# Attention output projection turned to channels on the partitions, and a second buffer for one tile of the S5 preparation

## The chip, the cores and the metric

The kernel runs on one core of a Trainium2 chip. The metric is the device time of one execution in microseconds; three executions of the kernel before were timed. One further execution was taken with the profiler and gives the trace that is quoted here.

## What is computed

One block on x of 1024 tokens by 1024 channels, in fp32. Cut to its main lines:

```python
h = rms_norm(x, norm1_g)
q, k, v, g_ret, u, g_s5 = split(h @ w_in)
ret = retention(rotary(q), rotary(k), v) * silu(g_ret)      # 8 heads, chunks of 128
ssm = s5_branch(u, ...) * silu(g_s5)                        # 64 groups of 16, state 64
x = x + concat([ret, ssm]) @ w_out
qa = rms_norm(x, norm2_g) @ xa_wq                           # 4 heads of 256
ka, va = m @ xa_wk, m @ xa_wv                               # m: 256 memory rows, normed
p = softmax(qa @ ka.T / 16)
x = x + (p @ va) @ xa_wo
return rms_norm(x, norm_f_g)
```

The S5 branch is computed with tables built from its parameters: powers of the state matrix, and the B and C matrices multiplied with them.

## The kernel before

Every projection is done in split precision: `mm3` (L100 to L103) issues three matmuls (high by high, high by low, low by high) for each block of 128 contracted channels. Weights come in groups of 256 columns through `load_w` (L71): SP issues two loads into `wraw`, ScalarE (ACT) copies the high part `whi`, VectorE (DVE) or GpSimd (POOL) subtracts the low part `wlo`. `get_w` always loads one group ahead.

The program's order is set by a list scheduler of the tile framework, separately for each engine: it uses its own durations, and every engine then works strictly in that order. SP issues nearly all DMAs, in order, so that one issue that waits holds all behind it. Tiles come from pools with a fixed number of buffers (`bufs`); a write waits until the readers of the buffer's last use are done.

The stages are: norm, then the loop `for i in range(4)` over pairs of retention heads (L612, about 0 to 400 us), then the u projection and S5 scan, the gates and the two parts of `w_out`, memory keys and values, queries and scores, and last the output projection `w_xo`.

**S5 preparation in the loop.** In the loop's iterations 1 to 3 a hook (`s5_hook`, L504) is called at fixed places. For each of 16 blocks b, `s5_prep(b)` (L457) computes W1 and VV on DVE with one product t1 on POOL (L476), and `s5_finish(b)` (L484) transposes W1 on TensorE (PE) into PSUM, `mps`, L488, and multiplies VV with B1, `kps`, L495. For each pair of blocks `s5_tables(ct)` (L422), ct 0 to 7, builds a 512 KB table on POOL by doubling (`tab`, L426 to L326), stores it with SP to `tab_d` (L430), stores a block of zeros from `z` (L432, L433), and computes B1, B2 and C1 on POOL (L447 to L454). `tab` and B1 have one buffer each, so the next `tab` waits for the store of the last, and the next B1 for the `kps` matmuls that read the last. The profile and the order drop digits from names: `B` is B1 on L447 to L450 and B2 on L451 to L453, `t` on L476 is t1, `C` is C1. In the order's rows a first number is the ct or the block b, and a last one is the tile's own number.

**The loop's other work around it.** `rope_load` (L296) copies the projected queries or keys from PSUM and swaps 32-row blocks with four SP DMAs (`sw_q`, `sw_k`, L303). `rope_turn` (L306) multiplies and adds on DVE (L309 to L311). `ret_store` (L593) transposes the retention output of the iteration before (`rtps`, L599), scales it on DVE (`rt`, L601) and stores it to `ret_d` (L604). `mps`, `kps`, `rtps` and other small PSUM tiles share one pool of four buffers.

**Output projection.** `wo_half(half, ...)` (L1020) works on 512 tokens. Tokens stand on the PSUM partitions: the attention output `o` is the stationary operand and 256 weight columns move, 768 matmuls of 128x256 over both halves. x1 lies in DRAM with channels on the partitions, so 64 PE transposes (`pxps`, L1038) and ACT copies turn it. DVE adds (L1048), ACT squares with a running sum along the row (L1050), and `finish` (L1057 to L1069) takes the reciprocal root for each 128 tokens, scales and stores. `attend(1, gi)` is interleaved with half 0. The lines around the sum:

```python
mm3(ps[:, t, 0:256], oT[k][0][:, ts], oT[k][1][:, ts], hi[:, k, :], lo[:, k, :], k == 0, k == 7)
v.tensor_tensor(x2[:, cs], ps[:, t, 0:256], x2[:, cs], ALU.add)
s.activation(jk, x2[:, cs], AF.Square, accum_out=ssq[t0 + t][:, gi:gi + 1])
```

Of the kernel before, what the change touches and what calls it, by code (L numbers as in the profile page):

```python
# [41 lines left out]
GELU_S = math.sqrt(2.0 / math.pi)  # L42
CONST_PAD, SSM_PAD, SB_PAD, KA_PAD, QA_PAD, PP_PAD, WO_OFF = 56, 16, 16, 8, 16, 48, 0


@with_exitstack
def block_kernel(ctx: ExitStack, tc: tile.TileContext, a: dict):
# [15 lines left out]
    def sm_ps(shape, name="smps"):  # L63
        return psm.tile(shape, F32, tag="sm", name=name)
# [82 lines left out]
    g2, gm, glu_b, invf, rsgn, nsgn, psgn = (off[z] for z in ("g2", "gm", "glu_b", "invf", "rsgn", "nsgn", "psgn"))  # L147
    d4, i16 = off["d4"], off["i16"]
    g1 = gp1
# [272 lines left out]
    def s5_tables(ct):  # L422
# [12 lines left out]
        sh = [P, 2, GB, 16]  # L435
        B1 = pr.tile([P, 2 * GB + 1, 16], F32, tag="B1", name=f"B1_{ct}")
        B2 = pr.tile([P, 2 * GB, 16], F32, tag="B2", name=f"B2_{ct}")
        C1 = pr.tile([P, 2 * GB, 16], F32, tag="C1", name=f"C1_{ct}")
        tt = pr.tile([P, 2, GB, 16], F32, tag="tt16", name=f"tt16_{ct}")
# [4 lines left out]
        def hg(x):  # L444
            return x.rearrange("p (h g) q -> p h g q", h=2)
# [7 lines left out]
        g.tensor_tensor(b2, b2, tt, ALU.subtract)  # L453
        g.tensor_scalar(hg(C1), raw[:, :, 2], psgn, None, op0=ALU.mult)  # L454
        per_ct[ct] = raw, B1, B2, C1

    def s5_prep(b):  # L457
        gs = slice(b * GB, b * GB + GB)
        ct, hb = b // 2, b % 2
        if hb == 0:  # L460
            s5_tables(ct)
        raw, B1, B2, C1 = per_ct[ct]
        ks = slice(hb * GB, hb * GB + GB)
        raw, B2, C1 = raw[:, hb], B2[:, ks], C1[:, ks]
# [12 lines left out]
        v.tensor_tensor(W1, W1, t1, ALU.add)  # L477
        v.tensor_tensor(VV, pw(PR, 9), ve(C1, 9), ALU.mult)
        v.tensor_tensor(t2, pw(PI, 9), ve(raw[:, 3], 9), ALU.mult)
# [539 lines left out]

    def wo_half(half, oT, between):  # L1020
        on = [qap.tile([P, D], F32, tag=("qhi", "qlo")[t % 2], name=f"on{half}{t}") for t in range(4)]
        ssq = [small.tile([P, 5], F32, tag=f"ssq{t}", name=f"ssq{half}{t}") for t in range(4)]
        pre = [z[:, 4:5] for z in ssq]
        for gi in range(4):
            hi, lo = get_w("w_xo", gi)
            xts = []
            for c in range(2):
                xt = pp.tile([P, 512], F32, tag="xt", name=f"xt{half}{gi}{c}", bufs=4)
                nc.sync.dma_start(out=xt, in_=a["x1_d"][2 * gi + c][:, half * 512:half * 512 + 512])
                xts.append(xt)  # L1030
            between(gi)
            cs = slice(gi * 256, gi * 256 + 256)
            for t0 in range(0, 4, 2):
                px = sm_ps([P, 2, 256], "pxps")
                for t in range(2):
                    ts = slice((t0 + t) * P, (t0 + t + 1) * P)
                    for c in range(2):
                        nc.tensor.transpose(px[:, t, c * P:c * P + P], xts[c][:, ts], ident)  # L1038
                    s.activation(on[t0 + t][:, cs], px[:, t, :], AF.Copy)
                ps = big_ps([P, 2, 512], "wops")  # L1040
                for t in range(2):
                    ts = slice((t0 + t) * P, (t0 + t + 1) * P)
                    for k in range(8):
                        mm3(ps[:, t, 0:256], oT[k][0][:, ts], oT[k][1][:, ts], hi[:, k, :], lo[:, k, :],
                            k == 0, k == 7)
                for t in range(2):
                    x2 = on[t0 + t]
                    v.tensor_tensor(x2[:, cs], ps[:, t, 0:256], x2[:, cs], ALU.add)  # L1048
                    jk = pp.tile([P, 256], F32, tag="jk", name="jk", bufs=2)
                    s.activation(jk, x2[:, cs], AF.Square, accum_out=ssq[t0 + t][:, gi:gi + 1])  # L1050
                    if gi < 3:
                        v.tensor_tensor(x2[:, cs], x2[:, cs], gf[:, cs], ALU.mult)
                    if gi == 2:
                        v.tensor_reduce(pre[t0 + t], ssq[t0 + t][:, 0:3], axis=AX.X, op=ALU.add)
                        v.tensor_scalar(pre[t0 + t], pre[t0 + t], 1.0 / D, EPS, op0=ALU.mult, op1=ALU.add)
                    if gi == 3:
                        finish(half, t0 + t, x2, ssq[t0 + t][:, 3:4], pre[t0 + t])  # L1057

    def finish(half, t, x2, last, pre):
        ss = small.tile([P, 1], F32, tag="ssf", name="ssf")  # L1060
        rf = small.tile([P, 1], F32, tag="rf", name="rf")
        v.scalar_tensor_tensor(ss, last, 1.0 / D, pre, op0=ALU.mult, op1=ALU.add)
        rsqrt(rf, ss, 1, "f")
        row = (half * 4 + t) * P
        s.activation(x2[:, 0:512], x2[:, 0:512], AF.Copy, scale=rf)
        nc.sync.dma_start(out=a["out"][row:row + P, 0:512], in_=x2[:, 0:512])
        v.scalar_tensor_tensor(x2[:, 768:D], x2[:, 768:D], rf, gf[:, 768:D], op0=ALU.mult, op1=ALU.mult)
        v.tensor_scalar(x2[:, 512:768], x2[:, 512:768], rf, None, op0=ALU.mult)
        nc.sync.dma_start(out=a["out"][row:row + P, 512:D], in_=x2[:, 512:D])  # L1069

# [28 lines left out]
def host_arrays(x, mem, positions, norm1_g, w_in, ret_gn_g, s5_a_re, s5_a_im, s5_log_dt,  # L1099
# [93 lines left out]
```

## Time and profile before

| what | value |
|---|---|
| median of 3 runs | 1151.91 us (1148.85 to 1152.83) |
| the profiled execution's own time | 1150.77 us |
| its span on the core | 1148.7 us |
| PE busy | 1118.4 us (97 %), 6636 matmuls |
| DVE, ACT, POOL busy | 654.8, 436.6, 241.0 us |
| mean granted clock of PE | 0.992 |
| HBM traffic | 122.04 MB read, 44.43 MB written |

The span runs from the first to the last instruction on the core. Times in the trace count from its start. The ends of matmuls are modelled, so the pace of PE is read from the distance between the starts of neighbouring matmuls, not from their durations.

### The profile page before, as it was taken

The page shows a single profiled execution, that of the slowest core. Times are in us where ns is not written, and L with a number is a line of the kernel's source. Part 1 is how long each engine was busy: PE and PEld are TensorE (multiplying, and loading weights), DVE is VectorE, ACT ScalarE, POOL GpSimd, SP SyncE. Part 2 cuts the span into 40 slices and gives each one's busy share as a digit, 9 for nine tenths or more (in the row PEclk, how much of TensorE's full clock was granted, in tenths as well). Part 3 has the DMA queues.
Part 4 walks back from the last instruction along what each step waited for, and adds up shares of the span by engine and source line. Part 5 has one row for each costly group of instructions (what it writes and reads, how often), then busy time and mean ns, then how long its engine had stood idle before and what let it go on. Part 6 is the DMA issues. An engine that isn't in the chain of part 4 may idle for free.

```text
span 1148.7 us, 17497 instructions
## 1 busy us (share of the span) xinstructions
PE 1118.4 (97%) x6636; PEld 966.3 (84%) x6636; DVE 654.8 (57%) x1388; ACT 436.6 (38%) x863; POOL 241.0 (21%) x342
## 2 busy tenths in 40 slices
PE   8999979999999999999999999999999999999996
PEld 6887957888888888887888888888889888889996
DVE  8896664765663445756585145443645555555564
ACT  7331422432432323434453133233334444344453
POOL 2338798452040001111121100002220000000000
PEclk9999989999999999999999999999999999999999
DMA  6413433442342299898794387443346422122251
GB/s 238 125 38 108 132 127 125 141 157 99 87 139 63 76 244 260 263 275 233 213 294 147 120 228 248 155 156 126 121 152 204 171 72 75 54 74 74 97 198 74
DMA packets 92372, 171.81 MB, mean 150 GB/s; under 512 B 10881, under 2 KB 46977, under 8 KB 92289
## 3 DMA queue, kind: packets, MB, share of 16 engines
q1 hardware_dynamic: 92000, 170.57, 47.2%
q8 instruction: 52, 0.85, 0.3%
q14 instruction: 32, 0.25, 0.1%
q10 hardware_dynamic: 288, 0.14, 0.0%
HBM read 122.04 MB, written 44.43 MB: 145 GB/s over the span
## 4 chain that ended last, share of the span: by engine, by line
PE 80%; POOL 8%; DMA 5%; DVE 4%; issue 1%; ACT 1%; SPq 0%; DVEq 0%; POOLq 0%; ACTq 0%
PE wops L101 3%; PE ups L103 3%; PE wops L103 3%; PE wops L102 3%; PE ups L101 3%; PE qaps L103 3%; PE qaps L102 3%; PE qaps L101 3%; PE obps L102 3%; PE ups L102 3%; PE obps L103 3%; PE glups L103 3%; PE obps L101 3%; PE glups L101 3%; PE glups L102 3%; PE gsps L101 2%
## 5 line engine op out<-in xcount | busy, mean ns | idle before, releaser
L102 PE MATMUL vps<-wlo_w_v,hh 128*128 128x256 f32 x256 | 73.0, 285 | 0.7 <-POOL wlo_w_v L81 0.7
L101 PE MATMUL vps<-whi_w_v,hh 128*128 128x256 f32 x256 | 73.0, 285 | 0.6 <-ACT qs_k L299 0.6
L101 PE MATMUL wops<-whi_w_xo,o 128*128 128x256 f32 x256 | 73.4, 287 | 0.0
L103 PE MATMUL vps<-whi_w_v,hl 128*128 128x256 f32 x256 | 73.0, 285 | 0.0
L103 PE MATMUL wops<-whi_w_xo,o 128*128 128x256 f32 x256 | 71.8, 280 | 0.0
L102 PE MATMUL wops<-wlo_w_xo,o 128*128 128x256 f32 x256 | 71.5, 279 | 0.0
L917 POOL TENSOR_TENSOR sq<-sq,sqx 128x1024 f32<-128x1024 f32 x7 | 19.2, 2738 | 195.3 <-ACT sqx L916 195.3
L101 PE MATMUL gsps<-hh,whi_w_gs 128*128 128x512 f32 x128 | 51.1, 399 | 0.0
L101 PE MATMUL gps<-hh,whi_w_g 128*128 128x512 f32 x128 | 51.0, 399 | 0.0
L101 PE MATMUL ups<-hh,whi_w_u 128*128 128x512 f32 x128 | 50.8, 397 | 0.0
L103 PE MATMUL ups<-hh,wlo_w_u 128*128 128x512 f32 x128 | 50.6, 395 | 0.0
L102 PE MATMUL gps<-hl,whi_w_g 128*128 128x512 f32 x128 | 50.6, 395 | 0.0
L102 PE MATMUL gsps<-hl,whi_w_gs 128*128 128x512 f32 x128 | 50.5, 395 | 0.0
L102 PE MATMUL ups<-hl,whi_w_u 128*128 128x512 f32 x128 | 50.4, 394 | 0.0
L103 PE MATMUL gps<-hh,wlo_w_g 128*128 128x512 f32 x128 | 50.4, 393 | 0.0
L103 PE MATMUL gsps<-hh,wlo_w_gs 128*128 128x512 f32 x128 | 50.3, 393 | 0.0
L101 PE MATMUL oaps<-reth,whi_w_oa 128*128 128x512 f32 x128 | 50.3, 393 | 0.0
L103 PE MATMUL qaps<-h,wlo_w_xq 128*128 128x512 f32 x128 | 50.2, 392 | 0.0
L101 PE MATMUL qaps<-h,whi_w_xq 128*128 128x512 f32 x128 | 50.1, 392 | 0.0
L102 PE MATMUL oaps<-retl,whi_w_oa 128*128 128x512 f32 x128 | 50.0, 391 | 0.0
L102 PE MATMUL qaps<-h,whi_w_xq 128*128 128x512 f32 x128 | 50.0, 390 | 0.0
L102 PE MATMUL obps<-ssmlo,whi_w_ob 128*128 128x512 f32 x128 | 49.9, 390 | 0.0
(394 smaller groups left out, 3372.6 us busy)
## 6 DMA issues: line engine op xcount, KB each, us to landing
CS<-tab_d SPq DMA_DIRECT2D x32, 256.0 KB, 5.9
yr<-y_d SPq DMA_DIRECT2D x16, 512.0 KB, 6.9
wraw_w_xq<-w_xq SPq DMA_DIRECT2D x16, 512.0 KB, 4.1
wraw_w_xo<-w_xo SPq DMA_DIRECT2D x16, 512.0 KB, 4.3
vv_d<-VV SPq DMA_DIRECT2D x16, 288.0 KB, 2.6
VV<-vv_d SPq DMA_DIRECT2D x16, 288.0 KB, 5.1
wraw_w_v<-w_v SPq DMA_DIRECT2D x8, 512.0 KB, 4.3
wraw_w_g<-w_g SPq DMA_DIRECT2D x8, 512.0 KB, 5.1
```

Of the source, the lines that this page charges most:

```text
L101: nc.tensor.matmul(out, wh, xh, start=first, stop=False)
L102: nc.tensor.matmul(out, wh, xl, start=False, stop=False)
L103: nc.tensor.matmul(out, wl, xh, start=False, stop=last)
L917: g.tensor_tensor(sq2, sq2, sq, ALU.add)
```

## The change

Two edits. First, the output projection has model channels on the PSUM partitions, and tokens move: 512 at a time in half 0 and for the first two weight groups of half 1, 256 at a time for groups 2 and 3 of half 1, in the order (2, first 256 tokens), (3, first), (2, second), (3, second). x1 is added as it lies in DRAM. The sum of squares goes over partitions now: ACT squares into `sqo`, POOL (DVE for group 3) adds into `acc`, PE sums by `mean_sq`, and PE spreads the reciprocal root over the partitions into PSUM (`rbps`). `token_rms` and `write_out` of one piece are called within the next piece's work. The output has the shape (8, 128, 1024) on the chip and the host turns it. The final gain is a column of 8 in the constants' tile `cp`, and the load of a broadcast row of 512 KB is gone. Second, B1 has two buffers, and the sign product is written in place into `bcraw` instead of the tile C1. Paddings are set anew.

```diff
-CONST_PAD, SSM_PAD, SB_PAD, KA_PAD, QA_PAD, PP_PAD, WO_OFF = 56, 16, 16, 8, 16, 48, 0
+CONST_PAD, SSM_PAD, SB_PAD, KA_PAD, QA_PAD, PP_PAD, WO_OFF = 48, 16, 16, 8, 16, 48, 16
...
-        B1 = pr.tile([P, 2 * GB + 1, 16], F32, tag="B1", name=f"B1_{ct}")
+        B1 = pr.tile([P, 2 * GB + 1, 16], F32, tag="B1", name=f"B1_{ct}", bufs=2)
...
-        C1 = pr.tile([P, 2 * GB, 16], F32, tag="C1", name=f"C1_{ct}")
...
-        g.tensor_scalar(hg(C1), raw[:, :, 2], psgn, None, op0=ALU.mult)
+        g.tensor_scalar(raw[:, :, 2], raw[:, :, 2], psgn, None, op0=ALU.mult)
...
-        v.tensor_tensor(VV, pw(PR, 9), ve(C1, 9), ALU.mult)
+        v.tensor_tensor(VV, pw(PR, 9), ve(raw[:, 2], 9), ALU.mult)
...
-    gf = ap_.tile([P, D], F32, name="gf")
-    nc.sync.dma_start(out=gf, in_=a["gf"].to_broadcast([P, D]))
...
+    def wo_half(half, oT, between, before=None):
+        x2, ws, xts = [], [], []
+        acc = pp.tile([P, 512], F32, tag="acc", name=f"acc{half}", bufs=2)
+        full, ta, tb = slice(0, 512), slice(0, 256), slice(256, 512)
+        for gi, ts in ([(z, full) for z in range(4)] if half == 0 else
+                       [(0, full), (1, full), (2, ta), (3, ta), (2, tb), (3, tb)]):
...
+            hi, lo = ws[gi]
+            ps = big_ps([P, 2, 512], "wops")
             for c in range(2):
...
+                cs = slice(c * P, c * P + P)
+                for k in range(8):
+                    mm3(ps[:, c, ts], hi[:, k, cs], lo[:, k, cs], oT[k][0][:, ts], oT[k][1][:, ts], k == 0, k == 7)
+                xo = x2[gi][:, c, ts]
+                v.tensor_tensor(xo, ps[:, c, ts], xts[2 * gi + c][:, ts], ALU.add)
+                if gi == 0 and c == 0:
+                    s.activation(acc, xo, AF.Square)
+                else:
+                    sq = pp.tile([P, 512], F32, tag="sqo", name=f"sqo{half}{gi}{c}", bufs=2)
+                    s.activation(sq[:, ts], xo, AF.Square)
+                    (v if gi == 3 else g).tensor_tensor(acc[:, ts], acc[:, ts], sq[:, ts], ALU.add)
+                if before and c == 0:
+                    before = token_rms(*before)
+                elif before:
+                    write_out(*before)
+                    before = None
+            if gi == 3:
+                before = (half, ts, x2, acc)
+        return before
+
+    def token_rms(half, ts, x2, acc):
+        n = (ts.stop - ts.start) // P
...
+        mean_sq(msf[:, :n], acc[:, ts], n, "f")
+        rsqrt(rf[:, :n], msf[:, :n], n, "f")
+        return half, ts, x2, rf
+
+    def write_out(half, ts, x2, rf):
+        n = (ts.stop - ts.start) // P
+        rb = sm_ps([P, 512], "rbps")
+        for j in range(n):
+            nc.tensor.matmul(rb[:, j * P:j * P + P], bc(rf[:, j:j + 1], [P, P]), ident, start=True, stop=True)
+        for ct in range(8):
+            xo = x2[ct // 2][:, ct % 2, ts]
+            v.scalar_tensor_tensor(xo, xo, gfc[:, ct:ct + 1], rb[:, 0:n * P], op0=ALU.mult, op1=ALU.mult)
+            nc.sync.dma_start(out=a["out"][ct][:, half * 512 + ts.start:half * 512 + ts.stop], in_=xo)
...
-    wo_half(0, oT0, lambda gi: attend(1, gi, pr1[gi], oT1))
-    wo_half(1, oT1, lambda gi: None)
+    last = wo_half(0, oT0, lambda gi: attend(1, gi, pr1[gi], oT1))
+    last = wo_half(1, oT1, lambda gi: None, last)
+    write_out(*token_rms(*last))
```

How the scheduler's order moves is shown at three places.

POOL, the kernel before, inside the table of ct 4 (`tab_2636`): the rows that complete B1 and B2 of ct 1 and then the product t1 of block 2 (`t_2`).

```order
L326 TENSOR_TENSOR tab_2636<-tab_2636,tg_2639 128x4x16
L454 TENSOR_SCALAR C_2_1892<-bcraw_1862,cp 128x128
L452 TENSOR_TENSOR tt_1_1679<-bcraw_1648,FI 128x128
L321 TENSOR_TENSOR tg_2639<-tab_2636 128x128
L324 TENSOR_TENSOR tab_2636<-tab_2636 128x4x32
L453 TENSOR_TENSOR B_1_1677<-B_1_1677,tt_1_1679 128x128
L322 TENSOR_TENSOR tab_2636<-tab_2636,tg_2639 128x4x32
L476 TENSOR_TENSOR t_2_1689<-PI,B_1_1677 128x512
```

So t1 of block 2 comes behind the last rows of B1 and B2 of ct 1, which themselves stand within this table. In the changed kernel, on POOL inside the table of ct 3 (`tab_2303`):

```order
L321 TENSOR_TENSOR tg_2306<-tab_2303 128x128
L324 TENSOR_TENSOR tab_2303<-tab_2303 128x4x32
L322 TENSOR_TENSOR tab_2303<-tab_2303,tg_2306 128x4x32
L325 TENSOR_TENSOR tg_2306<-tab_2303 128x128
L475 TENSOR_TENSOR t_2_1687<-PI,B_1_1676 128x512
L320 TENSOR_TENSOR tab_2303<-tab_2303 128x4x64
```

The product for block 2 stands one table earlier, and all rows of B1 and B2 of ct 1 now stand ahead of the first table. In turn, on POOL of the changed kernel from the end of the table of ct 5 (`z_2868`) into the table of ct 6 (`tab_3286`):

```order
L432 MEMSET z_2868 128x224
L451 TENSOR_TENSOR tt_3_2331<-bcraw_2301,FI 128x128
L426 COPY tab_3286<-rotC 128x4x16
L475 TENSOR_TENSOR t_5_2186<-PI,B_2_1889 128x512
L427 COPY tab_3286<-rotS 128x4x16
L320 TENSOR_TENSOR tab_3286<-tab_3286 128x4x16
L450 TENSOR_TENSOR B_3_2330<-bcraw_2301,FRs 128x128
L453 TENSOR_SCALAR bcraw_2630<-bcraw_2630,cp 128x2x64
L324 TENSOR_TENSOR tab_3286<-tab_3286 128x4x16
L452 TENSOR_TENSOR B_3_2330<-B_3_2330,tt_3_2331 128x128
L321 TENSOR_TENSOR tg_3289<-tab_3286 128x64
L448 TENSOR_TENSOR tt_4_2660<-bcraw_2630,FIs 128x128
```

Of these, t1 of block 5 and the first product of B2 of ct 3 (L450) stood in this table before too; the sign product and `tt_4` stood behind the last table, as did the other five rows for B1 and B2 of ct 3, three of which now stand just ahead of this piece and two in it. That makes seven more rows ahead of the last table's end. SP, the changed kernel, around the last table's store (`tab_3615` is the table of ct 7): the query swaps of iteration 2 (`sw_q`) stand behind it, as they did.

```order
L430 DMA tab_d<-tab_3615 128x1024
L433 DMA k_d<-z_3638 128x2x112
L490 DMA mi_d<-Mi_2172 128x512
L499 DMA k_d<-K_2181 128x128
L491 DMA vv_d<-VV_2342 128x576
L76 DMA wraw_w_kq_80_2681<-w_kq 128x1024
L303 DMA sw_q_2246<-qs_q_2244 32x1024 x4
```

In the order of the kernel before the same seven stand in the same sequence, with other buffer numbers; nothing moved here.

DVE, the changed kernel, from the last addition of the last projection tile to the end: `x_first` to `x_13` are the four pairs of channel tiles, 128x256 tokens; the first eight scalings belong to the third piece of tokens, the second eight to the last.

```order
L1041 TENSOR_TENSOR x_13_9920<-wops,xt_9923 128x256
L1072 SCALAR_TENSOR_TENSOR x_first<-x_first,cp,rbps 128x256 x2
L1072 SCALAR_TENSOR_TENSOR x_11_9768<-x_11_9768,cp,rbps 128x256 x2
L1072 SCALAR_TENSOR_TENSOR x_12_9844<-x_12_9844,cp,rbps 128x256 x2
L1072 SCALAR_TENSOR_TENSOR x_13_9920<-x_13_9920,cp,rbps 128x256 x2
L1047 TENSOR_TENSOR acc_9651<-acc_9651,sqo_10131 128x256
L284 TENSOR_SCALAR msf<-ms_f 128x2
L121 TENSOR_SCALAR i_f<-msf 128x2
```

The addition of the last squares to `acc`, from which the last root follows, stands behind the eight scalings of the piece before. On PE the spreading matmuls of that piece stand behind the last projection matmul:

```order
L103 MATMUL wops<-o_9591,wlo_w_xo_54_9846 128x256
L1069 MATMUL rbps<-cp,rf 128x128 x2
L283 MATMUL ms_f<-ones,acc_9651 128x1 x2
L1069 MATMUL rbps<-cp,rf 128x128 x2
L1190 UNCONDITIONAL_BRANCH
```

Before, the last projection matmul was the last work of PE.

## Rows read from the trace of the kernel before

**Rows 1.** Waits of PE: engine line, waited for, us in total, times, longest us.

```profile
PE mps L488 <- DVE W L477: 8.3, 1, 8.3
...
PE yps L741 <- POOL wlo_w_gs L81: 1.9, 1, 1.9
```

**Rows 2.** Timeline of POOL and PE, 158 to 167 us: start, length (us), instruction, [idle, releaser].

```profile
158.23 1.63 POOL L454 TENSOR_SCALAR C<-bcraw,cp 128x128 f32<-128x128 f32 x1
...
163.28 1.10 POOL L476 TENSOR_TENSOR t<-PI,B 128x512 f32<-128x512 f32 x1
...
165.43 1.09 PE L488 MATMUL mps<-cp,W 128*128 128x128 f32 x4 [8.35 <-DVE W L477]
```

**Rows 3.** Windows: stretch, busy us (count) of PE, PEld, DVE, ACT, POOL, clock, DMA.

```profile
165.00:170.00 5.00, 4.57 (x19) 3.31 (x20) 4.93 (x7) 1.82 (x3) 5.00 (x7) 0.50 0.31 115
```

**Rows 4.** Timelines of SP, POOL, DVE and PE, 215 to 233 us.

```profile
215.55 0.33 SPq L430 DMA_DIRECT2D tab_d<-tab  x1
...
217.81 0.43 SPq L492 DMA_DIRECT2D vv_d<-VV  x1
220.53 0.33 SPq L76 DMA_DIRECT2D wraw_w_kq<-w_kq  x1
221.12 2.62 SPq L303 DMA_DIRECT2D sw_q<-qs_q  x4
...
215.58 0.29 POOL L432 MEMSET z<- 128x224 f32 x1
...
227.17 1.23 DVE L310 TENSOR_TENSOR sw_q<-sw_q,sinT 128x1024 f32<-128x1024 f32 x1 [0.43 <-DMA sw_q<-qs_q]
...
229.45 0.74 DVE L601 SCALAR_TENSOR_TENSOR rt<-rtps,cp,silu 128x512 f32<-128x512 f32 x1
...
232.79 0.60 PE L488 MATMUL mps<-cp,W 128*128 128x128 f32 x4
```

**Rows 5.** Timeline of POOL: the same step of two tables, at 125 and at 156 us.

```profile
125.56 0.75 POOL L324 TENSOR_TENSOR tab<-tab 128x64 f32<-128x64 f32 x1
...
155.97 0.30 POOL L324 TENSOR_TENSOR tab<-tab 128x64 f32<-128x64 f32 x1
```

**Rows 6.** Timeline of PE: queries (512 moving), output projection of half 0 and half 1.

```profile
914.98 0.39 PE L101 MATMUL qaps<-h,whi_w_xq 128*128 128x512 f32 x1
915.21 0.39 PE L102 MATMUL qaps<-h,whi_w_xq 128*128 128x512 f32 x1
...
1061.67 0.28 PE L101 MATMUL wops<-whi_w_xo,o 128*128 128x256 f32 x1
1061.79 0.28 PE L102 MATMUL wops<-wlo_w_xo,o 128*128 128x256 f32 x1
...
1091.63 0.28 PE L102 MATMUL wops<-wlo_w_xo,o 128*128 128x256 f32 x1
1091.74 0.28 PE L103 MATMUL wops<-whi_w_xo,o 128*128 128x256 f32 x1
1091.86 0.38 PE L1038 MATMUL pxps<-cp,xt 128*128 128x128 f32 x2
1092.00 0.36 PE L101 MATMUL wops<-whi_w_xo,o 128*128 128x256 f32 x1
1092.20 0.28 PE L102 MATMUL wops<-wlo_w_xo,o 128*128 128x256 f32 x1
```

**Rows 7.** Timeline of the end, 1139 us to the end of the span, PE, DVE and SP.

```profile
1139.29 0.28 PE L103 MATMUL wops<-whi_w_xo,o 128*128 128x256 f32 x1
1139.60 0.76 DVE L1048 TENSOR_TENSOR on<-wops,on 128x256 f32<-128x256 f32 x2 [0.86 <-PE wops L103]
...
1143.07 0.48 DVE L1067 SCALAR_TENSOR_TENSOR on<-on,rf,gf 128x256 f32<-128x256 f32 x1
1143.47 0.35 DVE L1068 TENSOR_SCALAR on<-on,rf 128x256 f32<-128x256 f32 x1
...
1145.20 0.41 SPq L1069 DMA_DIRECT2D out<-on  x1
```

More of the change, by code (lines that the diff above doesn't have):

```diff
@@ L147, in block_kernel @@
     g2, gm, glu_b, invf, rsgn, nsgn, psgn = (off[z] for z in ("g2", "gm", "glu_b", "invf", "rsgn", "nsgn", "psgn"))
-    d4, i16 = off["d4"], off["i16"]
+    d4, i16, gfc = off["d4"], off["i16"], off["gf"]
     g1 = gp1
@@ L453, in s5_tables @@
         g.tensor_tensor(b2, b2, tt, ALU.subtract)
-        g.tensor_scalar(hg(C1), raw[:, :, 2], psgn, None, op0=ALU.mult)
-        per_ct[ct] = raw, B1, B2, C1
+        g.tensor_scalar(raw[:, :, 2], raw[:, :, 2], psgn, None, op0=ALU.mult)
+        per_ct[ct] = raw, B1, B2
     def s5_prep(b):
@@ L461, in s5_prep @@
             s5_tables(ct)
-        raw, B1, B2, C1 = per_ct[ct]
+        raw, B1, B2 = per_ct[ct]
         ks = slice(hb * GB, hb * GB + GB)
-        raw, B2, C1 = raw[:, hb], B2[:, ks], C1[:, ks]
+        raw, B2 = raw[:, hb], B2[:, ks]
         def pw(tab, n):
@@ L1018, in attend @@
             lst.append((hi, lo))
[L1020 to L1026, printed above, removed]
-            for c in range(2):
[L1028 to L1069, printed above, removed]
+    def wo_half(half, oT, between, before=None):
[4 more added lines that the diff above has]
+                       [(0, full), (1, full), (2, ta), (3, ta), (2, tb), (3, tb)]):
+            if gi == len(ws):
+                if half and gi == 0:
+                    x2.append(pp.tile([P, 2, 512], F32, name="x2_first"))
+                else:
+                    x2.append(qap.tile([P, 2, 512], F32, tag=("qhi", "qlo")[gi % 2], name=f"x2_{half}{gi}"))
+                ws.append(get_w("w_xo", gi))
+                for c in range(2):
+                    xt = pp.tile([P, 512], F32, tag="xt", name=f"xt{half}{gi}{c}", bufs=4)
+                    nc.sync.dma_start(out=xt, in_=a["x1_d"][2 * gi + c][:, half * 512:half * 512 + 512])
+                    xts.append(xt)
+                between(gi)
+            hi, lo = ws[gi]
+            ps = big_ps([P, 2, 512], "wops")
+            for c in range(2):
+                cs = slice(c * P, c * P + P)
[5 more added lines that the diff above has]
+                    s.activation(acc, xo, AF.Square)
+                else:
+                    sq = pp.tile([P, 512], F32, tag="sqo", name=f"sqo{half}{gi}{c}", bufs=2)
[9 more added lines that the diff above has]
+        return before
@@ new lines, in token_rms @@
+    def token_rms(half, ts, x2, acc):
+        n = (ts.stop - ts.start) // P
+        msf = small.tile([P, 4], F32, tag="msf", name="msf")
+        rf = small.tile([P, 4], F32, tag="rf", name="rf")
+        mean_sq(msf[:, :n], acc[:, ts], n, "f")
[10 more added lines that the diff above has]
+            nc.sync.dma_start(out=a["out"][ct][:, half * 512 + ts.start:half * 512 + ts.stop], in_=xo)
@@ L1090 @@
 CPACK = (("ident", 128), ("cmask", 128), ("gv", 8), ("geps", 8), ("g128", 4), ("gn_g", 8), ("g2", 8), ("gm", 8),
-         ("glu_b", 8), ("invf", 1), ("rsgn", 1), ("nsgn", 1), ("psgn", 1), ("d4", 16), ("i16", 16))
+         ("glu_b", 8), ("invf", 1), ("rsgn", 1), ("nsgn", 1), ("psgn", 1), ("d4", 16), ("i16", 16), ("gf", 8))
 CPW = sum(z for _, z in CPACK)
@@ L1128, in host_arrays @@
     out["gn_g"] = col(np.asarray(ret_gn_g)[0])
-    out["gf"] = c(np.asarray(norm_f_g).reshape(1, D))
+    out["gf"] = col(norm_f_g)
     out["glu_b"] = col(np.asarray(s5_glu_b)[0][chp])
@@ L1183 @@
            for n, z in arrays.items()}
-    aps["out"] = nc.dram_tensor("out", (L, D), F32, kind="ExternalOutput").ap()
+    aps["out"] = nc.dram_tensor("out", (8, P, L), F32, kind="ExternalOutput").ap()
     with tile.TileContext(nc, schedule_with_timeline_sim=True) as tc:
@@ L1190 @@
     out = np.empty((L, D), np.float32)
-    out[tok_perm()] = np.asarray(r.results[0]["out"])
+    out[tok_perm()] = np.asarray(r.results[0]["out"]).reshape(D, L).T
     return out.reshape(1, L, D)
```

## The prediction

> **What bounds the kernel.** I read the page's totals first: PE is busy for 97 % of the span, so time can come only from PE's work, from the few places where PE stands still, or from the stretch behind its last matmul. The list of PE's waits shows the largest of the first kind: the transposes of S5 block 2 waited 8.3 us for DVE's W [rows 1]. The timeline tells why: POOL, inside the table of ct 4, was still completing B1 and B2 of ct 1, with a sign product of 1.63 us among them, and t1, on which W hangs, started only at 163.28; PE resumed at 165.43 [rows 2]. The windows add a second price of that wait: PE came back at a granted clock of 0.50, the lower level, and had done 4.57 us of work in the window to 170 at that rate, of which half, 2.3 us, is lost [rows 3]. For the end I read the timeline behind the last matmul: it starts at 1139.29, the span ends at 1148.7, so 9.1 us follow its end at 1139.57 [rows 7].
>
> **The S5 edit: what goes.** With a second buffer for B1, its rows for ct 1 go ahead of the first table and t1 of block 2 into the table of ct 3, the one ahead of the table in which it stood. W of block 2 is then ready before PE asks at 157.08 (165.43 less 8.35). Gone: 8.3 + 2.3 = 10.6 us, if nothing else holds PE.
>
> **The S5 edit: what is late next.** PE would now reach everything behind 165 some 10 us sooner. One thing does not move with it: the transposes of block 5 (232.79) take a PSUM buffer of the small pool that is released by the first `rt` of iteration 2, a DVE operation that started at 229.45 and ended at 230.19, behind the swapped queries' product at 227.17, which itself waited for SP's swaps [rows 4]. These stand on SP behind the last table's store, which POOL's table releases at 215.55. So block 5 hangs on POOL's tables, not on PE.
> - How late are the tables? The order puts seven more POOL rows (128x128 products and sums, one sign product) ahead of the last table's end. Their like takes 0.3 to 0.6 us, so some 3 us. Bounds: 2 us if they are all short; 3 and another 2 to 3 if they fall beside wide DVE work: the same 128x64 step of a table took 0.75 us at 125.56, beside the rope's products, against 0.30 us at 155.97 [rows 5]. I take the store at 218.5 to 221.
> - From the store to the swaps' issue, SP took 5.6 us (215.55 to 221.12), of which 2.3 us was a wait for the weight buffer, from the end of the issue at 217.81 to 220.53 [rows 4]; without it 3.3. From swap issue to product 6.05 us (221.12 to 227.17), from there to the end of `rt` 3.0 us (227.17 to 230.19). Sum 12.3 us behind the store, so `rt` ends at 230.8 to 233.3.
> - Then PE's matmuls for block 5 run at about 231 to 233.5, against 232.79. The 10 us gained at 157 are waited out ahead of 232: **nearly all is given back**. I take 232.3, that is -0.5.
> - A wait of several us can bring the halved clock again: 0 if the wait is broken into short ones, 2.3 if it is one like that at 157 [rows 3]. I take 0.8, nearer to the short ones, since POOL and SP are late at several earlier places too (the table stores ahead of `k_d`, the rotated keys) and cut the gain in pieces.
> S5 in sum: +0.3, between -4 (short POOL rows, other buffer order) and +5 (POOL late by the upper bound, clock halved).
>
> **The projection: removed.** 64 transposes of x1. The stretch from 1091.63 to 1092.20 holds three matmul slots and two transposes: 0.57 - 3 x 0.113 = 0.23 us for two, 0.115 each [rows 6], together 64 x 0.115 = 7.4 us. All of it is on PE's path: **-7.4**. The ACT copies, the row multiplications on DVE and the load of the gain row lay beside PE; they are worth nothing.
>
> **The projection: the wider moving tile.** 384 pairs of 256-wide matmuls become 288 of 512 and 192 of 256. By distance of starts, 256 columns take 0.113 (1091.63 to 1091.74) and 0.12 in half 0 (1061.67 to 1061.79, where attention matmuls are mixed in), 512 columns take 0.23 (914.98 to 915.21) [rows 6]. Durations (0.28 and 0.39) are modelled and mislead. In half 1 that is 96 x (2 x 0.113 - 0.227) = 0; in half 0 it is 192 x (0.24 - 0.23) = **-1.9**, and 0 if the 512-wide ones lose as much beside the attention. The Trainium skill, "TensorE: Matmul & The Clock Gate", section "Back-to-back issue gap", gives sustained spacings of about 81 ns for 128 and 131 ns for 512 columns; by these a 512-wide matmul costs much less than two of 256, and the sum would be some 19 us lower (an estimate from that page, with a 256-wide one at 98 ns on the line between: 288 x 65 ns). The queries' spacing of 0.23 us at 512 columns speaks against it here, so it stays a rival of small chance.
>
> **Added on PE.** Six sums of squares and four spreading matmuls lie in the stream ahead of the last projection matmul; the nearest narrow ones, four transposes of `mps`, took 0.60 us, 0.15 each [rows 4]: **+1.5**, at least 1.0.
>
> **Weight hand-over.** Each weight group's copy must still follow the release by the group two before. Before, PE lost nothing there. The new DVE and ACT orders start these copies a little later, and little slack is left. Lower bound 0, upper bound two waits like the 1.9 us that PE spent for a late low part of a weight [rows 1], 4 us. I take **+1**, nearer to no wait.
>
> **The end.** Before: add at 1139.60, first scaling at 1143.07, so 3.5 us for squares and root; four scalings and products to about 1144.7; last store issued at 1145.20; 3.5 us to the end [rows 7]. After, the order puts eight scalings of the third piece between the last addition and the last sum of squares, at 0.40 us spacing (1143.07 to 1143.47): +3.2. Two trips through PE (sum, spread) take the place of ACT's running sum: some +0.8, between 0.3 and 1.5. Eight scalings stand where four operations stood: +1.6. Together **+5.6**, between 4 and 7. POOL's additions to `acc` have a whole matmul group of some 11 us of cover each; without it they would add 1 to 2 us each.
>
> **Sum** against the profiled execution of 1150.77: 0.3 - 7.4 - 1.9 + 1.5 + 1.0 + 5.6 = -0.9, 1149.9. The median of the runs lies 1.1 above that execution, so I forecast 1151.0.
>
> **Rivals.**
> 1. *The S5 gain holds.* If POOL's tables are not later than before (the seven rows lie where POOL waits for a store anyway) and SP's weight buffer is free sooner, the store goes at 210 to 215.5, `rt` ends 12.3 later, at 222 to 228, and PE keeps 5 to 10 us. For it: the wait on SP of 2.3 us is DVE's doing and moves with PE. Against: seven rows of work do not vanish, and the step at 155.97 already ran at the short time [rows 5]. Time 1141 to 1146; chance 0.24.
> 2. *Slower.* The last table comes later than 221 because more of it falls beside wide DVE work [rows 5]. From there each us of POOL is a us of PE: at 224, `rt` ends at 236.3, PE loses 3.5 against before, and 2.3 for the clock [rows 3], which is 1151.0 + 4.0 + 1.5 = 1156.5. The point from which it decides is a store at about 223 (or, to the same time, two weight hand-overs of 1.9). For it: the rows that moved meet the rope's products of iteration 2. Against: the last table's store of before, at 215.55, already stood behind such work. Time 1155 to 1158; chance 0.24.
> 3. *Wide tiles are cheaper.* If a 512-wide matmul cost only as much more as the durations show, 0.39 to 0.28 [rows 6], half 0 would take 192 x 0.12 x 1.39 = 32 instead of 46 and the wide part of half 1 15 instead of 22: 21 us less, 1130. Chance 0.02, by the queries' spacing.
> That the change does not do what it says is ruled out by the order: the transposes are gone and t1 stands a table earlier.
>
> **How the numbers follow.** A measurement of this kernel tells about 0.3 % (3.5 us) from no change. The forecast case has 0.50, spread over 1147 to 1155: 0.41 of it within 0.3 %, 0.06 faster, 0.03 slower. With rivals 1 and 3 faster has 0.32, with rival 2 slower 0.27. The range takes in most of rival 1 and of rival 2: 1141 to 1157; the forecast case alone gives 1147 to 1155.
>
> **What would show it.** In the trace after: no wait at 157 for block 2; in its place waits of PE between 175 and 235, together about 10 us, the largest before block 5's transposes or the `rt` chain; the last table's store at 218 to 221. No `pxps`; 512-wide `wops` at 0.227 to 0.23; 14 to 15 us behind the last projection matmul, of which eight scalings are 3.2. The prediction is wrong if block 5's transposes start well before 229 or after 236, if PE waits for weights in the last stage by more than 4 us, or if the wide matmuls start closer than 0.22.

## The result, and the profile after

The changed kernel takes 1165.93 us in the median of four runs (1164.61 to 1167.82), the kernel before 1151.13 beside it. The ratio is 1.0131, with a 95 % interval of 1.0107 to 1.0155: slower by some 15 us, where 1151.0 and a range of 1141 to 1157 were forecast.

The profiled execution took 1165.47 us, with a span of 1163.7. Set against the trace of before by the starts of the first `ups`, the first `wops` and the last `wops`, it divides like this:

| stretch | before, us | after, us | difference | forecast |
|---|---|---|---|---|
| start to the first `ups` (loop with S5) | 356.70 | 360.40 | +3.7 | +0.3 |
| first `ups` to first `wops` | 669.61 | 669.56 | 0 | 0 |
| first to last `wops` | 112.98 | 118.20 | +5.2 | -6.8 |
| last `wops` to the end | 9.41 | 15.54 | +6.1 | +5.6 |

The list of PE's waits has new entries (columns as in [rows 1]: us in total, times, longest us):

```profile
PE mps L487 <- DVE rt L600: 12.2, 1, 12.2
PE wops L101 <- DVE x L1041: 7.1, 4, 5.8
PE ms_f L283 <- DVE acc L1047: 3.7, 1, 3.7
...
PE mps L487 <- DVE W L476: 1.5, 1, 1.5
```

The 8.3 us of block 2 [rows 1] are gone. In their place stand 12.2 us for `rt`, and the projection has waits of its own, which the forecast did not have.

**The loop.** The timelines of the changed kernel at the places of [rows 4] and just ahead (POOL, then SP, then DVE and PE; `...` stands for rows left out):

```profile
210.87 0.34 POOL L321 TENSOR_TENSOR tg<-tab 128x64 f32<-128x64 f32 x1 [1.74 <-DMA k_d<-z]
...
213.81 1.53 POOL L322 TENSOR_TENSOR tab<-tab,tg 128x128 f32<-128x128 f32 x1
215.42 1.27 POOL L325 TENSOR_TENSOR tg<-tab 128x128 f32<-128x128 f32 x1
216.65 1.59 POOL L320 TENSOR_TENSOR tab<-tab 128x256 f32<-128x256 f32 x1
...
205.29 0.32 SPq L430 DMA_DIRECT2D tab_d<-tab  x1
205.70 2.46 SPq L303 DMA_DIRECT2D sw_k<-qs_k  x4
208.26 0.53 SPq L433 DMA_DIRECT2D k_d<-z  x1
222.15 0.33 SPq L430 DMA_DIRECT2D tab_d<-tab  x1
...
225.40 2.42 SPq L303 DMA_DIRECT2D sw_q<-qs_q  x4
...
213.81 1.21 DVE L309 TENSOR_TENSOR rot_k<-qs_k,cosT 128x1024 f32<-128x1024 f32 x1
...
232.06 1.23 DVE L310 TENSOR_TENSOR sw_q<-sw_q,sinT 128x1024 f32<-128x1024 f32 x1 [14.30 <-DMA sw_q<-qs_q]
...
234.34 0.74 DVE L600 SCALAR_TENSOR_TENSOR rt<-rtps,cp,silu 128x512 f32<-128x512 f32 x1
...
235.14 1.11 PE L487 MATMUL mps<-cp,W 128*128 128x128 f32 x4 [12.19 <-DVE rt L600]
```

The chain is the forecast one, step for step: last table's store at 222.15, swaps 3.25 us later, product 6.66 later, end of `rt` 3.0 after that, PE at once. What was too small is its first number: the store came at 222.15, where 218.5 to 221 was taken. Of the 6.6 us against the kernel before, 2.0 are there when the last table begins (its first copy starts at 208.17, for 206.16 before). Two things on POOL add the rest. Three of its operations fell beside DVE's wide rope products (from 213.81 on) and took 4.39 us, 2.9 more than the same three of the last table of before:

```profile
209.41 0.45 POOL L322 TENSOR_TENSOR tab<-tab,tg 128x128 f32<-128x128 f32 x1
209.94 0.40 POOL L325 TENSOR_TENSOR tg<-tab 128x128 f32<-128x128 f32 x1
210.30 0.61 POOL L320 TENSOR_TENSOR tab<-tab 128x256 f32<-128x256 f32 x1
```

And POOL waited 1.74 us for the store of the zeros of the table before, which SP issued at 208.26, behind four `sw_k` swaps: the tile of zeros shares its buffer with the table's scratch. In the kernel before, this store stood ahead of the swaps (203.85 and 204.33). So SP's order did move, one table ahead of the piece of it that was shown.

The windows behind it show PE's return at half clock (columns as in [rows 3]):

```profile
230.00:235.00 5.00, 0.00 (x0) 0.00 (x0) 2.94 (x3) 0.00 (x0) 0.00 (x0) 0.50 0.40 116
235.00:240.00 5.00, 4.86 (x34) 4.53 (x35) 4.90 (x8) 0.87 (x2) 1.11 (x3) 0.69 0.60 225
```

At a mean of 0.69 the second window lost 1.5 us (4.86 x 0.31).

**The projection.** The timelines of DVE and PE of the changed kernel in half 1, at its first tile of 256 tokens:

```profile
1112.70 5.36 DVE L1072 SCALAR_TENSOR_TENSOR x<-x,cp,rbps 128x512 f32<-128x512 f32 x8 [1.31 <-PE rbps L1069]
1117.97 1.01 DVE L1041 TENSOR_TENSOR x<-wops,xt 128x256 f32<-128x256 f32 x2
...
1118.44 0.58 PE L101 MATMUL wops<-o,whi_w_xo 128*128 128x256 f32 x1 [5.78 <-DVE x L1041]
1118.82 0.41 PE L102 MATMUL wops<-o,whi_w_xo 128*128 128x256 f32 x1
```

And its windows there:

```profile
1115.00:1120.00 5.00, 1.56 (x7) 1.56 (x8) 3.98 (x7) 0.63 (x1) 0.15 (x1) 0.53 1.00 370
1120.00:1125.00 5.00, 5.00 (x26) 4.60 (x26) 0.00 (x0) 0.00 (x0) 1.12 (x1) 0.78 0.16 52
```

PE stands for 5.78 us, behind eight scalings of half 0, which take 5.36 us on DVE, and then one addition. It comes back at half clock once more (1.56 x 0.47 + 5.00 x 0.22 = 1.8 us). Why PE waits for an addition at all is told by the program: the code issues column 0's 24 matmuls, its addition, then column 1's matmuls, all into one PSUM tile, and in the trace the first matmul of column 1 is released by the addition that reads column 0 (e3 below takes this order away). In the kernel before both tokens' matmuls stand ahead of both additions. In most groups the scheduler had put another tile's matmuls between; in the last groups of half 1 it had none, and there the same wait shows three more times as a gap of 0.68 to 0.80 us between starts.

**The end.** Behind the last projection matmul (start 1148.16, the last row of `wops`), to be held against [rows 7]:

```profile
1148.16 0.28 PE L103 MATMUL wops<-o,wlo_w_xo 128*128 128x256 f32 x1
...
1148.92 0.87 DVE L1072 SCALAR_TENSOR_TENSOR x_first<-x_first,cp,rbps 128x256 f32<-128x256 f32 x2
...
1152.06 0.42 DVE L1047 TENSOR_TENSOR acc<-acc,sqo 128x256 f32<-128x256 f32 x1
1152.63 0.75 PE L283 MATMUL ms_f<-ones,acc 128*128 128x1 f32 x4 [3.74 <-DVE acc L1047]
1153.42 0.16 DVE L284 TENSOR_SCALAR msf<-ms_f 128x2 f32<-128x2 f32 x1 [0.94 <-PE ms_f L283]
...
1157.13 0.87 DVE L1072 SCALAR_TENSOR_TENSOR x_first<-x_first,cp,rbps 128x256 f32<-128x256 f32 x2 [1.38 <-PE rbps L1069]
```

Eight scalings from 1148.92 to about 1152.1, sum, root, eight scalings from 1157.13: as forecast, and 0.5 us longer in all.

### The profile page after: what moved, and what is told of

It is laid out like the page before. It is cut to its first block, busy times and chain, and to the rows that moved or that the text cites. A ratio compares the mean times of both kernels' runs of the same rounds, so it can differ in the third digit from the quotient of the medians.

```text
span 1163.7 us, 16711 instructions
## 1 busy us (share of the span) xinstructions
PE 1117.5 (96%) x6316; PEld 952.7 (82%) x6316; DVE 657.4 (56%) x1290; ACT 415.5 (36%) x779; POOL 259.8 (22%) x354
## 4 chain that ended last, share of the span: by engine, by line
PE 71%; DMA 11%; POOL 7%; DVE 6%; issue 2%; ACT 1%; SPq 1%; DVEq 0%; ACTq 0%
PE wops L101 3%; PE ups L103 3%; PE wops L102 3%; PE ups L101 3%; PE qaps L103 3%; PE qaps L102 3%; PE wops L103 3%; PE qaps L101 3%; PE ups L102 3%; PE obps L102 3%; PE obps L101 3%; PE glups L102 2%; PE obps L103 2%; PE glups L101 2%; PE glups L103 2%; PE oaps L103 2%
## 5 line engine op out<-in xcount | busy, mean ns | idle before, releaser
L1047 POOL TENSOR_TENSOR acc<-acc,sqo 128x512 f32<-128x512 f32 (+1 forms) x12 | 15.6, 1303 | 261.2 <-issue 188.4
L101 PE MATMUL wops<-o,whi_w_xo 128*128 128x512 f32 (+1 forms) x160 | 56.9, 356 | 7.1 <-DVE x L1041 7.1
L102 PE MATMUL wops<-o,whi_w_xo 128*128 128x512 f32 (+1 forms) x160 | 56.4, 353 | 0.0
L103 PE MATMUL wops<-o,wlo_w_xo 128*128 128x512 f32 (+1 forms) x160 | 56.0, 353 | 0.0
L101 PE MATMUL obps<-ssmhi,whi_w_ob 128*128 128x512 f32 x128 | 49.9, 390 | 0.0
```

The costliest lines, as they stand in the source:

```text
L101: nc.tensor.matmul(out, wh, xh, start=first, stop=False)
L102: nc.tensor.matmul(out, wh, xl, start=False, stop=False)
L103: nc.tensor.matmul(out, wl, xh, start=False, stop=last)
L1047: (v if gi == 3 else g).tensor_tensor(acc[:, ts], acc[:, ts], sq[:, ts], ALU.add)
```

## The experiments

The ratios below are against the kernel before, timed in turn with the variant on the same chip; its own median differed from one set of runs to another (1148 to 1150). The theory at the outset, A: the two edits cost separately, the S5 edit by a wait for `rt`, the projection by the wait for an addition and by the longer end. The rivals stand in the expectations that are printed with each run.

### e1: the S5 edit alone

The kernel before with the S5 lines of the change, and nothing else (two of them are shown; the others drop the tile C1 and let VV read `bcraw`):

```diff
-        B1 = pr.tile([P, 2 * GB + 1, 16], F32, tag="B1", name=f"B1_{ct}")
+        B1 = pr.tile([P, 2 * GB + 1, 16], F32, tag="B1", name=f"B1_{ct}", bufs=2)
-        g.tensor_scalar(hg(C1), raw[:, :, 2], psgn, None, op0=ALU.mult)
+        g.tensor_scalar(raw[:, :, 2], raw[:, :, 2], psgn, None, op0=ALU.mult)
```

> The kernel before with the S5 edit alone. Theory A (the two edits cost separately; the S5 edit trades the wait of block 2 for one of block 5 behind the retention scaling rt): 1154.5 us, 3.4 above before, between 1153 and 1156; the wait of mps for rt is about 12 us again and the wait at 157 us is gone. Rival B (the S5 edit by itself is a gain, and only the shifted buffers of the whole change spoil it): 1140 to 1144, no wait of mps above 3 us.

Measured: 1.0045 (1.0021 to 1.0068), 5 us slower. PE's longest wait:

```profile
PE mps L487 <- DVE rt L600: 11.4, 1, 11.4
```

No wait for W stands in the list. Theory A holds; the edit, meant for the wait at 157, moved it to 225 and made it longer. The trace of e1 also has half clock from 99 to 109 us, which that of the changed kernel has not (last section).

### e2: the projection alone

The changed kernel with B1 and C1 as before (the lines of e1 taken back).

> The changed kernel with B1 and C1 as before, so the projection edit alone. Theory A: 1151.1 + 5.2 in the stage + 6.4 behind its last matmul = 1162.7, between 1160.5 and 1165; the wait of mps for W is 8.3 again, the wait of wops for the addition 7 us as in the changed kernel. Rival B (the projection edit is near neutral in itself and suffers from S5 only): 1150 to 1153.

Measured: 1.0102 (1.0066 to 1.0137), 12 us slower. From its waits:

```profile
PE mps L488 <- DVE W L477: 8.2, 1, 8.2
PE wops L101 <- DVE x L1042: 7.1, 4, 5.8
```

The two ratios, 1.0045 and 1.0102, make 1.0147 together, and the whole change has 1.0131 (1.0107 to 1.0155): they add.

### e3: matmuls of both columns first

```diff
                 for k in range(8):
                     mm3(ps[:, c, ts], hi[:, k, cs], lo[:, k, cs], oT[k][0][:, ts], oT[k][1][:, ts], k == 0, k == 7)
+            for c in range(2):
                 xo = x2[gi][:, c, ts]
```

> The changed kernel with the matmuls of both columns of a tile issued ahead of its additions. Theory A (the second column's first matmul waits for the first column's addition out of the same PSUM tile, and that addition stands behind eight scalings on DVE): the waits of wops for x go from 7.1 us to under 1, with some 2 us of half clock and three hand-overs of 0.57: 1165.9 - 5.8 - 1.9 - 1.7 = 1156.5, between 1155 and 1159. Rival B (the stage is slow by late weights or by the pace of the wide matmuls): 1164 to 1167, the same distance of first to last wops, 118 us.

Measured: 1.0097 (1.0063 to 1.0131), against 1.0131 for the whole change: 4 us of the expected 9. In the trace the stage from first to last `wops` is 112.4 instead of 118.2 us, so 5.8 went there, and the end is 1.0 longer. The wait for x is gone from the list. One of 2.5 us, put down to ACT's `sqo`, has come; by the times a later tile waits for a PSUM buffer whose additions still stand on DVE behind the scalings. Three matmuls behind it the clock fell:

```profile
1120.00:1125.00 5.00, 2.52 (x15) 2.34 (x14) 3.41 (x7) 1.65 (x3) 1.91 (x2) 0.83 0.48 166
```

Sixteen matmuls of 256 columns started 0.20 to 0.21 us apart there, which cost 1.5 us. A was right on the cause and too high on the sum: it counted the wait and its half clock as wholly gone, and left out the end.

### e4: the swaps issued by ACT

```diff
-            nc.sync.dma_start(out=sw[32 * b:32 * b + 32, :], in_=qs[o:o + 32, :])
+            nc.scalar.dma_start(out=sw[32 * b:32 * b + 32, :], in_=qs[o:o + 32, :])
```

> The changed kernel with the swaps of queries and keys issued by ACT instead of SP. Theory A (block 5 waits for rt, rt for the queries' product, that for SP, which stands behind the last table's store): the wait of mps for rt falls from 12.2 us to under 3 and 10 to 14 us go: 1152 to 1156. Rival B (block 5 is bound by POOL's tables themselves, or by another reader of them): the wait changes its name but stays, 1163 to 1167.

Measured: 1.0126 (1.009 to 1.0161), no gain that can be told. The wait for `rt` fell to 2.7 us, but this came in the trace:

```profile
214.57 10.45 ACTq L303 DMA_DIRECT2D sw_q<-qs_q  x3
...
221.18 0.32 SPq L430 DMA_DIRECT2D tab_d<-tab  x1
...
225.62 0.48 PE L598 MATMUL rtps<-cp,o 128*128 128x128 f32 x1 [5.28 <-ACT o L589]
```

(SP's row is of the last table.) ACT issued the first swap at 214.57, but the second only at 223.86, the third at 224.41 and the fourth at 226.76. The trace's semaphores say why. The DMAs of SP and ACT signal their end on the same eight counters, and a swap waits until the last user of its counter has landed. For the second that was the last table's store, which landed at 223.84, for the third the store of zeros (224.28), for the fourth that of `Mi` (224.91). So the queue changed and the order did not; now ACT's normalisation of `o` stood behind the swaps too. The time is that of rival B, and the experiment did not take away what it was meant to.

### e5, e6: the tables stored by POOL

In the trace of e5 POOL's DMAs report on eight other counters, so that neither SP nor ACT stands in their way:

```diff
-        nc.sync.dma_start(out=a["tab_d"][ct], in_=tab)
+        g.dma_start(out=a["tab_d"][ct], in_=tab)
-        nc.sync.dma_start(out=a["k_d"][ct].rearrange("(h p) t -> p h t", h=2)[:, :, 0:112], in_=zero)
+        g.dma_start(out=a["k_d"][ct].rearrange("(h p) t -> p h t", h=2)[:, :, 0:112], in_=zero)
```

On the changed kernel:

> The changed kernel with the stores of the S5 tables and of the zeros issued by POOL itself, so that neither SP nor the DMAs' shared completion counters of the other queues stand between a table and the queries' swaps. Theory A (block 5 hangs on the last table's store through the swaps): the swaps are issued 8 to 10 us earlier, the wait of mps for rt falls from 12.2 us to under 4, and 7 to 12 us go against the changed kernel, that is 1.003 of the kernel before, between 1.001 and 1.007. Rival B (the retention's own chain, its statistics and ACT's normalisation, is as late as the swaps, as the wait of rtps for o in the run with the swaps on ACT suggests): only 2 to 5 us go, 1.008 to 1.012, and a wait of rtps for o stands in its place.

On the kernel before with the S5 edit (e1):

> The kernel before with the S5 edit and the stores by POOL. Theory A: the wait of 8.3 us at 157 and its half clock are gone and nothing takes their place: 0.992 of the kernel before, between 0.989 and 0.996. Rival B: 0.998 to 1.004.

Measured: e5 1.0072 (1.0043 to 1.01), 7 us less than the whole change; e6 0.9971 (0.9945 to 0.9996), 8 us less than e1. In e5 the swaps left at 215.18 instead of 225.40:

```profile
215.18 2.44 SPq L303 DMA_DIRECT2D sw_q<-qs_q  x4
...
224.73 0.24 POOL L426 COPY tab<-rotC 128x64 f32<-128x64 f32 x1 [4.72 <-DMA tab_d<-tab]
...
234.85 1.10 POOL L475 TENSOR_TENSOR t<-PI,B 128x512 f32<-128x512 f32 x1
...
236.83 1.08 PE L487 MATMUL mps<-cp,W 128*128 128x128 f32 x4 [5.12 <-DVE W L476]
```

The wait for `rt` is gone and one of 5.1 us for W has taken its place (6.0 in e6): t1 of the next block, 6, stands on POOL behind the last table, and that table had itself waited 4.72 us for the store of the one ahead to land. So the swaps were one bound, and POOL's own sequence the next one, close behind. That was neither theory as written; rival B named the wrong place.

### e7: both repairs

> Both repairs on the changed kernel: stores by POOL, and the matmuls of both columns ahead of the additions. If they act in different stages they add: the ratio of the run with the matmuls first (1.0097) less what the stores by POOL take from the changed kernel. Theory A 1.000, between 0.997 and 1.003; rival B 1.004 to 1.008.

Measured: 1.0016 (0.9998 to 1.0035). Stage 110.9 us, end 16.9 us. The repairs act in different stages and add.

### e8: t1 on DVE

e6, and:

```diff
-        g.tensor_tensor(t1, pw(PI, 8), ve(B2, 8), ALU.mult)
+        v.tensor_tensor(t1, pw(PI, 8), ve(B2, 8), ALU.mult)
```

> The kernel before with the S5 edit, the stores by POOL, and the product t1 on DVE instead of POOL. Theory A (what was left in the run with the stores by POOL, a wait of 6.0 us of mps for W, is t1 of block 6 standing behind the last table on POOL): the wait goes, with its half clock, 6 to 9 us: 0.9971 - 0.006 = 0.991 of the kernel before, between 0.988 and 0.994. Rival B (DVE is now late, its 0.8 us more for each of 16 blocks stands in front of W): 0.996 to 1.001.

Measured: 0.99 (0.9868 to 0.9933), 1137.08 us in the median. In the list of waits nothing of S5 is left:

```profile
PE ops L566 <- DVE st L556: 2.4, 1, 2.4
PE wps L202 <- DVE zero L199: 1.5, 1, 1.5
PE yps L740 <- DVE X L736: 1.5, 1, 1.5
```

The first `ups` starts at 346.1, 10.6 us sooner than before. This version beats both kernels. It has the projection of before.

### e9: the third piece not scaled

In `write_out` of e7, no scaling and no store for the first 256 tokens of half 1:

```diff
-        for ct in range(8):
+        for ct in range(8 if ts.start or n == 4 else 0):
```

> The kernel with both repairs, without the eight scalings of the third piece of tokens and their stores (these outputs are left out). Theory A (the scalings stand on DVE between the last addition and the last sum of squares): the stretch from the start of the last projection matmul to the end of the span falls from 17.1 us by 3.2, to 13.9, between 13.4 and 14.4. Rival B (the end is set by the trips through PE at half clock and by the stores): less than 1.5 us go, 15.6 or more.

Measured: 1.0009 (0.9988 to 1.0031). The last `wops` starts at 1133.43 and the span ends at 1147.2: 13.8 us, 3.0 less than e7's 16.85. In the whole time it can't be told from e7 (1.0016). In the timeline the sum of squares now follows the addition at once (DVE, PE):

```profile
1133.75 0.76 DVE L1042 TENSOR_TENSOR x<-wops,xt 128x256 f32<-128x256 f32 x2 [2.21 <-PE wops L103]
...
1134.79 0.95 DVE L1048 TENSOR_TENSOR acc<-acc,sqo 128x256 f32<-128x256 f32 x2 [0.28 <-ACT sqo L1047]
1135.89 0.58 PE L283 MATMUL ms_f<-ones,acc 128*128 128x1 f32 x4 [1.73 <-DVE acc L1048]
```

The forecast's term for these scalings, 3.2, was about right. What is left is still 4.4 us longer than the end of before.

### e10: the kernel before without its transposes

The tiles of x1 are added as they lie, so the sums are of other elements; PE's other work is the same.

```diff
-                px = sm_ps([P, 2, 256], "pxps")
...
                     for c in range(2):
-                        nc.tensor.transpose(px[:, t, c * P:c * P + P], xts[c][:, ts], ident)
-                    s.activation(on[t0 + t][:, cs], px[:, t, :], AF.Copy)
+                        s.activation(on[t0 + t][:, gi * 256 + c * P:gi * 256 + c * P + P], xts[c][:, ts], AF.Copy)
```

> The kernel before with the 64 transposes of x1 left out (ACT copies the tiles of x1 as they lie, so the sum takes them untransposed). Theory A (they lie on the path of PE): 7.4 us go, from first to last wops 105.6 instead of 113.0, 0.9936 of the kernel before, between 0.992 and 0.9955. Rival B (PE hides half of them beside the loads of weights): 3 to 4 us, 0.9965 to 0.998.

Measured: 0.9958 (0.9938 to 0.9978). The stage is 107.4 us instead of 113.0: 5.6 us, between the theories. Two neighbours of the last part of half 1:

```profile
1128.10 0.28 PE L102 MATMUL wops<-wlo_w_xo,o 128*128 128x256 f32 x1
1128.22 0.28 PE L103 MATMUL wops<-whi_w_xo,o 128*128 128x256 f32 x1
```

They start 0.118 apart in the median of the last 30 us, where it was 0.113 in the kernel before. The median overstates it, since some pairs of before were slower: the mean of half 1 is 0.1178, for 0.1142 before between matmuls that stand behind no transpose. Over the 384 matmuls of half 1 that is 1.4 us lost again, which with 5.6 makes 7.0, close to the forecast 7.4. Why the spacing differs stays open.

### e11, e12: the projection beside a loop without waits, and the loop with one buffer

e11 is e7 with t1 on DVE; e12 is e8 with one buffer for B1 and the tile C1 as before.

> The changed kernel with the matmuls first, the stores by POOL and t1 on DVE, beside the same S5 loop with the projection of before (0.990). Theory A (with the matmuls first the projection's stage is 2.1 us shorter and its end 7.7 us longer than before, whatever the loop does): 0.990 + 0.005 = 0.995 of the kernel before, between 0.992 and 0.998. Rival B (the projection's loss came from what the loop left behind): 0.988 to 0.991.

Measured: 0.9943 (0.9928 to 0.9958). Stage 112.2, end 16.8 us: 0.8 us shorter and 7.4 longer than before. (The 1.3 us between this stage and e7's 110.9 are half clock behind the wait of 2.5 us, which e7 has at full clock.) With the same loop and the projection of before (e8) it is 0.99, so even the repaired projection costs about 0.4 %, 5 us, and it does so at the end. Theory A.

> The kernel before with the stores by POOL and t1 on DVE, but one buffer for B1 and the tile C1 as they were. Theory A (block 2 waits for B1 and B2 of ct 1, which a single buffer lets POOL begin only behind the kps matmuls of ct 0): a wait of 5 to 8 us at 157 stays, 0.996 to 1.000 of the kernel before. Rival B (the second buffer was not needed, t1 on DVE and the stores do it all): 0.988 to 0.992.

Measured: 1.0061 (1.0044 to 1.0078). Its longest waits:

```profile
PE mps L488 <- DVE W L477: 8.5, 1, 8.5
PE ops L567 <- DVE st L557: 5.2, 3, 3.2
```

The wait at 157 stays, so the S5 edit is what removes it, as theory A has it. Its time is above A's range: the waits for `st` are 5.2 us instead of 3.5, and behind the one of 3.2 us, which ends at 198, PE ran at half clock (0.50 from 200 to 205). Against e8 with 0.99, the S5 edit is worth 1.6 % once POOL is relieved. In the change alone it cost 0.45 % (e1). The second buffer and the sign product in place were not tried apart; that the gain is the buffer's follows from the order of POOL's rows and is not shown by a run.

## Why the prediction was wrong

**The S5 edit: what goes.** Right: the wait of block 2 and its half clock are gone.

**What is late next.** Right in mechanism, wrong in one size. That block 5 hangs on `rt`, `rt` on the swaps and the swaps on the last table's store is what the trace after shows and what e5 and e6 confirm. The first step failed: "I take the store at 218.5 to 221". It came at 222.15. The seven more rows were counted, at 3 us, and the last table began 2.0 late. The contention bound was taken only in part (2.9 us came), and the wait of POOL for the zeros (1.7 us) has no term, though SP's rows above have the `sw_k` swaps between a table's store and that of its zeros. Block 5's transposes started at 235.14 for 232.3, 2.8 us later, and the half clock cost 1.5 for 0.8: these are the +3.7 for +0.3. The store came between the forecast's 221 and the 223 from which rival 2 was to decide; what happened is of rival 2's kind, and its time of 1156.5 counted the S5 part alone. The bound of 0 for the clock behind short waits does not hold either: in e1 a wait of 2.8 us was followed by half clock (last section).

**The projection.** The step that failed is the sum of its stage, -7.4 - 1.9 + 1.5 + 1.0 = -6.8: it has no term for a wait of PE for additions. Measured +5.2, so 12.0 us are missing. 7.1 are the waits for x, 1.8 the half clock behind the longest. Of the rest, 0.9 is the sums and spreadings (2.4 us by the distance of starts, for 1.5), and 1.3 is a spacing of 0.120 for the 192 narrow matmuls of half 1, which was 0.113 before. Against that, the weight hand-over cost nothing, for +1.0. Of the remaining 1.9, some 1.1 lie in the saving: by the distance of starts `wops` and `pxps` took 96.0 us before, and the transposes and the wide tile gave 8.2 of it back (with the narrow matmuls at the old 0.113), for 9.3. The last 0.8 is mostly the restarts around the waits. The cost was to be seen in the code and the order: the addition of column 0 stands in the program ahead of column 1's matmuls into the same PSUM tile, and in DVE's order eight scalings of 0.67 us stand ahead of the addition. The scalings of half 0 and what waits behind them on DVE have no term in the prediction. This is the largest error.

**Removed transposes.** Right that they lie on PE's path, and near in size: 7.4 forecast, 5.6 measured in the stage, 7.0 with the changed spacing of the other matmuls put back (e10).

**The wide tile.** Right that the saving is small; the 1.9 us were read too high. The 0.12 us of half 0 came from one pair of neighbours [rows 6], and the median there is 0.117, by which 192 x (0.234 - 0.231) = 0.6. The 384 `wops` of half 0 take 45.3 us by the distance of starts in e10, the 192 of the changed kernel 44.3: 1.0 us. Neighbours of 512 columns in the changed projection:

```profile
1092.63 0.39 PE L101 MATMUL wops<-o,whi_w_xo 128*128 128x512 f32 x1
1092.85 0.39 PE L102 MATMUL wops<-o,whi_w_xo 128*128 128x512 f32 x1
1093.08 0.40 PE L103 MATMUL wops<-o,wlo_w_xo 128*128 128x512 f32 x1
```

0.22 to 0.23 us, so rival 3 is out, and the measurement decides against the sustained spacing of about 131 ns for 512 columns that the Trainium skill, "TensorE: Matmul & The Clock Gate", section "Back-to-back issue gap", states; that section's other figure, the isolated gap of N / 2.4 + 2.5 ns (216 for 512 columns), is the near one, 4 to 6 % below.

**The end.** Right: +5.6 forecast, +6.1 measured, 3.0 of it the eight scalings (e9).

Together: 3.4 from S5, 12.0 from the stage and 0.5 from the end are the 15.9 us between -0.9 and +15.0. None of the prediction's signs of being wrong came: block 5 at 235.14 lies between 229 and 236, no wait for weights stands in the last stage, and the wide matmuls start 0.227 us apart in the median. No sign looked at PE's waits for DVE in the projection.

## What to carry to other kernels

When the work that empties PSUM moves, follow the order of issue within one tile: here a matmul into the second part of a tile, issued behind the reader of the first, waited for that reader, and with it for everything ahead of that reader on its engine. When a buffer is added to relieve one wait, find what PE reaches next and on which engine's length it hangs; here the S5 edit was worth 1.6 % of the time with POOL relieved and cost 0.45 % without. Moving the swaps from SP to ACT broke no wait, because the two shared their counters; before moving a DMA, look at what it waits for.

## What the runs showed that was not expected

- The spacing of the same 128x256 matmuls takes values of 0.113, 0.118 and 0.120 us in different kernels and halves, with no wait in the list and a full clock; in e10 only transposes between them were left out. Over a half it is 1 to 3 us, and its cause is open.
- Behind its wait of 5.8 us in the projection PE came back at half clock, as behind the waits of 8 and 12 us in the loop. Short waits did it too, but not each time. Behind the wait of 2.5 us in the projection e3 and e11 fell to half clock, and e7 and e9 did not. Near 99 us PE waits for `st`: 2.82 us in the changed kernel, with the clock at 1.00 behind it, and 2.79 us in e1, with this window behind it:

```profile
100.00:105.00 5.00, 5.00 (x23) 4.04 (x22) 0.42 (x2) 0.00 (x0) 4.69 (x14) 0.50 0.18 43
```

So one trace of the loop can lose some us in a place where another, with the same wait, loses nothing. The ratios above rest on 4 to 10 executions of each variant, the stretches on one.
- Profiled executions of kernels with the same stretch differ by up to 5 us there (first `ups` to first `wops` 669.6 before and after, 664.6 to 667.1 in e1 to e4; before has half clock from 528 to 532, the others do not). A difference between single traces of that stretch says nothing on an edit elsewhere.
